# A hyena and gMLP encoder block on one core: ordinary products for the first two column pairs with the sine network as a background job, gate pairs and branch A last, and a last DFT step that multiplies standing data

## The chip, the cores and the metric
The kernel runs on one core of one Trainium2 chip. The metric is the device time of one execution in microseconds, lower is better. A core has a matrix engine (PE, whose loads of standing operands are listed as PEld), a vector engine (DVE), a scalar engine (ACT), a slower general engine (POOL), and SP, which here only issues transfers. Each engine takes its instructions in order.

## What is computed
One encoder layer on x of 2048 positions by 1024 channels:

```
h = rms_norm(x, pre_norm_w);  proj = h @ w_in            (1024 x 7168)
hy_in, hy_gate, sg_u, sg_v, sg_gate = split(proj)
A: x0, x1, v = split(short_conv(hy_in)); k = hyena_filter(...)   (a three layer sine network, times a decay)
   y_a = x0 * long_conv(v * x1, k, skip) * silu(hy_gate)         (by FFT)
B: y_b = sg_u * (sgu_w @ norm(sg_v) + sgu_b) * silu(sg_gate)     (per head and chunk of 128)
y = concat(y_a, y_b) @ w_out;  out = x + rms_norm(y, post_norm_w)
```

All is float32; the large products keep that accuracy by three passes with split operands (high parts and low parts).

## The kernel before
**Products.** The input and output products are cut into *pairs*: a pair takes two column blocks of 128 (two heads, or a gate with its operand) and half of the positions (h = 0 or 1, two chunks of 512). Each pair is a 2 by 2 block product done in Strassen's manner (the Winograd form): seven *units* u = 0 to 6, each a product of one combination of x (`self.X[u]`) and one combination of weights (a tile `wu`), each of 4 blocks times 3 passes: 84 matmuls of 128x512 a pair (`product`, `mm3`, lines 303 to 305 of the profile). `prep_begin` loads the two weight blocks as `wraw` and makes the combinations s1, s2, s3 (tiles `ws`, line 613); `prep_unit` makes high and low part of one unit's weights (lines 634 and 636); what is made in the first half of the positions is written to a spill (`WSB`, `WSU`, `WSG`, `WSV`) and read again in the second. `stream` runs the pairs in the order of `self.order`; the results leave PSUM in the `Take` classes.

**Order.** 72 pairs: for the first half of positions B (branch B's gate and operand), U (the two convolution inputs of branch A), V (branch B's values) mixed with G (branch A's gate); for the second half U, V mixed with G, B; then eight output pairs O for branch A (r = 0), whose sums go to `PT`, and eight for branch B (r = 1), which add them, normalise and write.

**Background.** Between the units, `tick` advances jobs; `background(jobs, rate)` starts so many a tick, with 3.5 ticks a pair. `x_phase` first normalises and turns the first half of x and makes all seven combinations; the sine network `mlp` stands ahead of the first pair in the program. Under the first eight pairs run the 32 filter jobs `k1_job` (decay, sums and differences, a first DFT step; lines 838 to 863, result `AK`), then `x_job` for the second half of x, `kfft_job`, `wo_job` (combinations of w_out, result `WT`), and under the second half's V, G and B pairs `fft_job` (two DFT steps and the product of the spectra, lines 1069 to 1085, result `BY`) and `inv_job` (the last step, lines 1101 to 1115, result `Y`). A scheduler then orders each engine's instructions; tiles come from pools with a fixed number of buffers for each tag, and a tile waits until the buffer's last user is done.

**The places that the change touches.** In `k1_job` the sums `s` have four buffers of their own (tag kq) and the evictions `ev` three. In `fft_jobs` the inverse jobs of the first channel half are mixed with the FFT jobs of the second. `inv_job` multiplies the table `g1`, standing, with the data (`b<-raw,g`, line 1107), copies the result on ACT (line 1109), turns it on PE (line 1113) and multiplies it on DVE with the gate (line 1114). When branch A's output pairs begin, `stream` lets all jobs end first (`turn`), since their weights are `Y`.

## Time and profile before

| | us |
|---|---|
| median of 3 runs | 2075.62 (2069.07 to 2076.07) |
| the profiled execution | 2072.21 |
| its span | 2070.2 |
| PE busy | 1904.2 (92%) |
| PE weight loads busy | 1414.1 (68%) |
| DVE busy | 1345.9 (65%) |
| ACT busy | 857.4 (41%) |
| POOL busy | 452.0 (22%) |

Matmuls are pipelined, so their times overlap and PE's busy share says little; the step from one start to the next says more. The transfers move 249 GB/s on the mean. A row of a group gives count, busy time, mean duration in ns, and the idle time of the engine ahead of the group with what ended it. A row of the table of stages gives a stretch, its length, and for each engine the busy time in it.

### The profile page before, as it was taken

Reading aid. Unit: us, or ns where it says so; the run is one execution under the profiler, and the core shown is the slowest. Engines: PE = TensorE matmul, PEld = TensorE weight load, DVE = VectorE, ACT = ScalarE, POOL = GpSimd, SP = SyncE. Lnnn points to the kernel's source line nnn. Section 1 sums busy time; section 2 is a strip of 40 time slices with the busy share of each in tenths; the row PEclk is TensorE's granted clock in tenths of the full one; section 3 lists DMA queues with packets and bytes.
Section 4 is the critical chain, followed back from the end, with each engine's and each line's share of the span. In section 5 each row is a group of like instructions: output and inputs, shape, how many; then the busy total and the mean of one; then the engine's idle time right before and its main releaser. Section 6 shows DMA issues by size and latency. Waiting matters only on the chain.

```text
span 2070.2 us, 23947 instructions
## 1 busy us (share of the span) xinstructions
PE 1904.2 (92%) x7832; PEld 1414.1 (68%) x7832; DVE 1345.9 (65%) x2070; ACT 857.4 (41%) x1540; POOL 452.0 (22%) x392
## 2 busy tenths in 40 slices
PE   4698899999999999899998999899999999999997
PEld 3465666777777777677776666566667777887776
DVE  6767878787755465745553888878672226536876
ACT  6344444565344443644444333233332224335443
POOL 4431322223212212121111111011011112323331
PEclk9899999999999999999999999899999999999999
DMA  8288777776687977998877797789898888536563
GB/s 272 105 262 268 244 247 259 232 261 242 237 292 233 342 227 272 324 281 256 274 247 234 243 303 258 218 281 286 273 294 291 280 268 290 188 102 244 193 213 132
DMA packets 330204, 515.91 MB, mean 249 GB/s; under 512 B 107451, under 2 KB 177339, under 8 KB 327359
## 3 DMA queue, kind: packets, MB, share of 16 engines
q1 hardware_dynamic: 263328, 439.58, 65.1%
q10 hardware_dynamic: 61856, 69.81, 9.9%
q0 software_dynamic: 4896, 4.98, 1.0%
q8 instruction: 63, 1.03, 0.2%
q14 instruction: 61, 0.50, 0.1%
HBM read 316.10 MB, written 204.48 MB: 251 GB/s over the span
## 4 chain that ended last, share of the span: by engine, by line
PE 33%; DVE 8%; DMA 6%; issue 2%; ACT 1%; POOL 1%; SPq 0%; DVEq 0%; ACTq 0%; POOLq 0%
PE proj L305 8%; PE proj L304 8%; PE proj L303 8%; PE b L1081 3%; PE b L1107 2%; PE b L1069 2%; DMA x<-WT 1%; DVE pb L1072 1%; DVE pa L1072 1%; DMA wraw<-Y 1%; DMA WT<-t 1%; DVE x L558 1%; DVE pa L1076 1%; PE b L996 1%; DVE wu L636 1%
## 5 line engine op out<-in xcount | busy, mean ns | idle before, releaser
L303 PE MATMUL proj<-x,wu 128*128 128x512 f32 x2016 | 833.0, 414 | 35.7 <-ACT sn L647 13.2
L304 PE MATMUL proj<-x,wu 128*128 128x512 f32 x2016 | 810.8, 402 | 12.8 <-DVE wu L636 10.3
L305 PE MATMUL proj<-x,wu 128*128 128x512 f32 x2016 | 807.6, 401 | 1.1 <-DVE x L558 0.6
L636 POOL TENSOR_TENSOR wu<-wraw,wu 128x512 fp32r<-128x512 f32 x172 | 262.3, 1525 | 1047.5 <-ACT wu L634 819.1
L303 PEld LDWEIGHTS proj<-x,wu 128*128 128x128 f32 x2016 | 383.6, 190 | 143.6 <-issue 33.7
L304 PEld LDWEIGHTS proj<-x,wu 128*128 128x128 f32 x2016 | 383.6, 190 | 118.2 <-issue 26.0
L305 PEld LDWEIGHTS proj<-x,wu 128*128 128x128 f32 x2016 | 383.4, 190 | 94.5 <-issue 13.5
L634 ACT CAST wu<-wraw 128x512 fp32r<-128x512 f32 x216 | 133.8, 620 | 285.5 <-PE proj L305 230.9
L636 DVE TENSOR_TENSOR wu<-ws,wu 128x512 fp32r<-128x512 f32 x176 | 129.8, 740 | 149.7 <-ACT wu L634 149.3
L634 ACT CAST wu<-ws 128x512 fp32r<-128x512 f32 x176 | 108.6, 620 | 219.5 <-PE proj L305 170.2
L647 ACT COPY sn<-proj 128x512 f32<-128x512 f32 x216 | 125.5, 581 | 109.5 <-PE proj L305 88.1
L1072 DVE TENSOR_TENSOR pa<-b,k 64x512 f32<-64x512 f32 x128 | 87.5, 683 | 51.2 <-PE b L1069 46.1
L613 POOL TENSOR_TENSOR ws<-wraw 128x512 f32<-128x512 f32 x44 | 80.3, 1825 | 161.1 <-DVE wu L636 113.1
L613 POOL TENSOR_TENSOR ws<-wraw,ws 128x512 f32<-128x512 f32 x44 | 59.4, 1350 | 220.9 <-DVE wu L636 212.5
L1072 DVE TENSOR_TENSOR pb<-b,k 64x512 f32<-64x512 f32 x128 | 88.9, 694 | 1.8
L1081 PE MATMUL b<-pa,tb 128*128 128x512 f32 x128 | 71.3, 639 | 14.4 <-DVE pa L1076 7.5
L1083 ACT COPY ev<-b 128x512 f32<-128x512 f32 x64 | 37.2, 585 | 108.0 <-PE b L1081 104.8
L613 DVE TENSOR_TENSOR ws<-wraw 128x512 f32<-128x512 f32 x44 | 40.4, 918 | 59.0 <-DMA wraw<-in_w_in_dram 24.9
L651 DVE TENSOR_TENSOR r<-proj,sn 128x512 f32<-128x512 f32 x64 | 43.8, 685 | 40.4 <-PE proj L305 39.6
L1069 PE MATMUL b<-raw,tu 128*128 128x512 f32 x128 | 66.0, 628 | 3.0 <-DMA raw<-AU 3.0
L861 PE MATMUL b<-s,ff 128*128 128x512 f32 x128 | 63.7, 613 | 5.0 <-ACT ev L863 2.3
L1032 PE MATMUL b<-raw,tk 128*128 128x512 f32 x128 | 63.6, 615 | 3.4 <-DMA raw<-AK 1.8
(169 smaller groups left out, 2234.8 us busy)
## 6 DMA issues: line engine op xcount, KB each, us to landing
wraw<-in_w_in_dram SPq DMA_DIRECT2D x84, 512.0 KB, 5.5
WSB<-wu SPq DMA_DIRECT2D x32, 512.0 KB, 4.9
dd<-in_c_dec_dram SPq DMA_DIRECT2D x32, 512.0 KB, 5.6
AK<-ev ACTq DMA_DIRECT2D x64, 256.0 KB, 4.2
WSU<-wu SPq DMA_DIRECT2D x32, 512.0 KB, 4.8
raw<-AK SPq DMA_DIRECT2D x32, 512.0 KB, 6.0
WSG<-wu SPq DMA_DIRECT2D x32, 512.0 KB, 6.3
KF<-ev ACTq DMA_DIRECT2D x32, 512.0 KB, 6.7
```

The source lines that it names most:

```text
L303: t.matmul(ps, sh, mh, start=first, stop=False, **kw)
L304: t.matmul(ps, sl, mh, start=False, stop=False, **kw)
L305: t.matmul(ps, sh, ml, start=False, stop=last, **kw)
L613: eng.tensor_tensor(t, x, y, op=op)
L634: nc.scalar.copy(w[:, 0], src[u])
L636: eng.tensor_tensor(w[:, 1], src[u], w[:, 0].bitcast(F32), op=ALU.subtract)
L647: self.nc.scalar.copy(s, ps)
L861: nc.tensor.matmul(ps, self.ff[:, d], s[d], start=True, stop=True)
L1032: nc.tensor.matmul(ps, tv[:, n], raw[:, n], start=True, stop=True)
L1069: nc.tensor.matmul(u, tv[0][:, n], raw[:, n], start=True, stop=True)
L1072: nc.vector.tensor_tensor(o, uu, kk, op=ALU.mult)
L1081: nc.tensor.matmul(ps, tv[1][:, n], prod[n], start=True, stop=True)
```

## The change
**First two pairs.** For the first two B pairs and the first half of positions the seven-unit product is replaced by the ordinary one: two block products for each output block, eight for a pair. `X[4]` and `X[6]` first hold the second chunk's plain blocks; the second pair's weights stand in `X[5]`'s place. The outputs go straight from PSUM through SiLU and a product to `UG`. What the second half needs of these pairs' combined weights is made apart (`first_sums`) from columns that are read a second time. `X[4]` and `X[5]` are filled afterwards. **Sine network.** It becomes one background job under the next two pairs, with a step after each layer's sine; the filter jobs follow under seven pairs, and `s`, `ev`, `wr`, `sk` share five buffers. **Order.** In the second half come U, then V mixed with B, then G, then the output pairs of branch B and last those of branch A. The FFT jobs run at 0.55 a tick, the inverse jobs all after them at 1.05, under the last G pairs and the branch B output pairs. **Last DFT step.** The data stand and the table moves, so the product comes out turned; the first PSUM bank, the ACT copy and the four turns go, and the gate tile moves from tag `ws` to `f`.

```diff
-        if self.h:
+        if not self.h:
             self.part = [self.b.o_load(2 * self.c + 1 - n) for n in range(2)][::-1]
...
-            self.order = B(0) + U(0) + GV(0) + U(1) + GV(1) + B(1) + O(0) + O(1)
+            self.order = B(0) + U(0) + GV(0) + U(1) + VB + G(1) + O(1) + O(0)
...
-                    self.nw_ = 3
+                    self.nw_ = 4
                     with self.pool("mlp") as ml:
-                        self.mlp(ml)
+                        self.background(iter([self.mlp(ml)]), 1.0)
+                        self.run(self.stream(2))
+                        self.rest()
                     with self.pool("k1") as kp:
-                        self.background(self.k1_jobs(kp), 1.4)
-                        self.run(self.stream(8))
+                        self.background(self.k1_jobs(kp), 1.6)
+                        self.run(self.stream(7))
...
-                    self.background(self.x_jobs(1), 0.25)
-                    self.run(self.stream(8))
+                    self.background(self.x_jobs(1), 0.32)
+                    self.run(self.stream(5))
...
-                    self.background(self.fft_jobs(), 1.0)
-                    self.run(self.stream(20, "w0"))
+                    self.background(self.fft_jobs(), 0.55)
+                    self.run(self.stream(20, "w1"))
+                    self.run(self.stream(8, "w0"))
...
+        def pair(n, chunk):
+            (b1, b2), c = ((0, 1), (4, 6))[chunk], self.order[n][2]
+            cols = slice(512 * chunk, 512 * chunk + 512)
+            sg, ps = None, None
+            for k in range(2):
+                ps = self.bank("proj")
+                self.product({0: X[b1]}, {0: w[n][2 * k]}, 0, ps, False)
+                yield
+                self.product({0: X[b2]}, {0: w[n][2 * k + 1]}, 0, ps, False, first=False)
+                if k == 0:
+                    sg = xs.tile([128, 512], F32, name="sg", tag="h", bufs=3)
+                    nc.scalar.activation(sg, ps, AF.Silu)
+                else:
+                    ug = xs.tile([128, 512], F32, name="ug", tag="h", bufs=3)
+                    nc.vector.tensor_tensor(ug, ps, sg, op=ALU.mult)
+                    nc.sync.dma_start(self.UG[c][:, cols], ug)
+                yield
...
+        for u, t, x, y, op in ((3, s1, a21, a22, ALU.add), (2, s2, s1, a11, ALU.subtract), (6, s1, a12, s2, ALU.subtract), (4, s2, a11, a21, ALU.subtract)):
+            tt(t, x, y, op=op)
+            spill(u, t)
+            yield
...
-        s = [kp.tile([128, 512], F32, name="s", tag="kq", bufs=4) for _ in range(2)]
+        s = [kp.tile([128, 512], F32, name="s", tag="kq", bufs=5) for _ in range(2)]
...
-            ev = kp.tile([128, 512], F32, name="ev", bufs=3)
+            ev = kp.tile([128, 512], F32, name="ev", tag="kq", bufs=5)
...
-        v = self.inv_jobs()
         for g in range(0, 32, 2):
             yield self.fft_job(g, 1)
-            if g > 6:
-                yield next(v)
-        for _ in range(4):
-            yield next(v)
-        yield iter(())
-        yield from v
+        for _ in range(2):
+            yield iter(())
+        self.rate = 1.05
+        yield from self.inv_jobs()
...
-        xg = self.product_tile("xg")
+        xg = self.f("xg")
...
-        ps = self.bank("b")
-        for d in range(2):
-            nc.tensor.matmul(ps, g1[:, d], raw[:, d], start=d == 0, stop=d == 1)
-        y = self.f("y")
-        nc.scalar.copy(y, ps)
-        yield
+
         ps = self.bank("a")
         for q in range(4):
-            nc.tensor.transpose(ps[:, q * 128:q * 128 + 128], y[:, q * 128:q * 128 + 128], self.ident)
+            sl = slice(q * 128, q * 128 + 128)
+            for d in range(2):
+                nc.tensor.matmul(ps[:, sl], raw[:, d, sl], g1[:, d], start=d == 0, stop=d == 1)
+        yield
```

On DVE, under the filter jobs, the program before had these rows (dd are the decayed columns, s their sum and difference, l their absolute sum, wu a weight's low part; in brackets the semaphores that a row waits for, DMAHW being transfers):

```order
L838 TENSOR_TENSOR dd<-a,dd 128x512 [waits PE_49]
L840 TENSOR_TENSOR s<-dd 128x512 [waits DVE_49]
L841 TENSOR_TENSOR s<-dd 128x512
L636 TENSOR_TENSOR wu<-ws,wu 128x512 [waits Activation_49]
L838 TENSOR_TENSOR dd<-a,dd 128x512 [waits DMAHW1_49,PE_49]
L843 TENSOR_TENSOR l_682<-l_682,dd 128x1024 [waits Activation_49]
```

The sums waited for DVE's own work alone, at all 64 places. In the changed program the same stretch of DVE reads:

```order
L947 TENSOR_TENSOR dd<-a,dd 128x512 [waits PE_49]
L949 TENSOR_TENSOR s<-dd 128x512 [waits DMAHW6_49,DMAHW0_49,DVE_49]
L950 TENSOR_TENSOR s<-dd 128x512 [waits PE_49]
L744 TENSOR_TENSOR wu<-ws,wu 128x512 [waits Activation_49]
L952 TENSOR_TENSOR l_1278<-l_1278,dd 128x1024 [waits Activation_49]
L947 TENSOR_TENSOR dd<-a,dd 128x512 [waits DMAHW2_49]
```

The buffer of a sum is now one that an eviction or a DFT product had, so 35 of the 64 sums wait for a transfer and others for PE. On PE, in the last DFT step, the program before had (proj products, b and a PSUM banks, pa and tb the second DFT step's operands, raw and tu the first one's):

```order
L303 MATMUL proj<-x_6863,wu 128x512
L1081 MATMUL b<-pa,tb 128x512
L1107 MATMUL b<-raw,g_10787 128x512 x2
L1069 MATMUL b<-raw,tu 128x512
L1113 MATMUL a<-ident,y 128x128 x4
L1069 MATMUL b<-raw,tu 128x512
L304 MATMUL proj<-x_6863,wu 128x512
```

The changed program has, under the branch B output pairs:

```order
L303 MATMUL proj<-x_13346,wu 128x512
L304 MATMUL proj<-x_13346,wu 128x512
L305 MATMUL proj<-x_13346,wu 128x512
L1217 MATMUL a<-g_13033,raw 128x128 x16
L303 MATMUL proj<-x_13374,wu 128x512
```

Sixteen rows of two jobs stand together, with no FFT row near them; the first stands after 4608 product matmuls of 6072, the last after 5328, and branch A's output pairs begin after 5400. On SP, where the second half's V pairs end, the changed program reads (VM is the mixed values' place in memory, vm the buffer that a B pair reads them into):

```order
L1078 DMA VM<-v_9324 128x1024 [waits DMAHW2_49,DVE_49]
L1070 DMA bi<-in_sgu_b_dram 128x128 [waits DMAHW3_49]
L713 DMA wraw<-in_w_in_dram 128x1024 [waits DMAHW4_49,Pool_49]
L174 DMA vm<-VM 128x1024 [waits DMAHW5_49,DMAHW2_49]
L738 DMA wu<-WSB_92 128x1024 [waits DMAHW6_49,PE_49]
```

The load of vm waits for the store three rows ahead of it (DMAHW2), whose buffer it takes; before, all V pairs of this half were over when the B pairs came.

More of the change, by code (lines that the diff above doesn't have):

```diff
@@ L440, in x_norm @@
         ss = xs.tile([128, 1], F32, name="ss", bufs=2)
-        jk = self.junk(xs)
+        jk = self.wide([128, D], "jk") if xs is self.fp else xs.tile([128, D], F32, name="jk")
         nc.scalar.activation(jk, xn, AF.Square, accum_out=ss)
@@ L485, in x_phase @@
             for i in range(4):
-                xts[c, i] = self.x_load(xs, 0, i, c, 4, nc.scalar if i % 2 else nc.sync)
+                xts[c, i] = self.x_load(xs, 0, i, c, 4, nc.scalar if i % 2 and not c else nc.sync)
                 if (c, i) == (0, 0):
                     nc.gpsimd.dma_start(pw, self.i["pre_norm_w"].partition_broadcast(128))
-                if (c, i) == (0, 3):
-                    self.next_w = self.prep_begin(0)
+                if (c, i) in ((0, 3), (1, 0)):
+                    self.first_weights(c)
         self.load_more()
+        X = self.X
+        hi = lambda u, i: X[u][:, 0, i]
+        lo = lambda u, i: X[u][:, 1, i]
         def put(u, src, i, eng):
-            hi, lo = self.X[u][:, 0, i], self.X[u][:, 1, i]
-            nc.scalar.copy(hi, src)
-            eng.tensor_tensor(lo, src, hi.bitcast(F32), op=ALU.subtract)
-        keep = {}
+            nc.scalar.copy(hi(u, i), src)
+            eng.tensor_tensor(lo(u, i), src, hi(u, i).bitcast(F32), op=ALU.subtract)
+        b11 = [self.rp.tile([128, 512], F32, name="b11", tag=t, bufs=n) for t, n in (("ws", 3), ("ws", 3), ("ws", 3), ("s1", 1))]
+        b21 = []
         for i in range(4):
@@ L504, in x_phase @@
                 put(half, ps, i, nc.vector)
-                keep[half, i] = xs.tile([128, 512], F32, name=f"b{half}", tag="b", bufs=8)
-                nc.scalar.copy(keep[half, i], ps)
+                if half:
+                    b21.append(xs.tile([128, 512], F32, name="b21", bufs=4))
+                    nc.vector.tensor_copy(b21[i], ps)
+                else:
+                    nc.scalar.copy(b11[i], ps)
+            if i == 1:
+                w = [self.first_split(0, [self.wp.tile([128, 2, 512], F32R, name="wu", tag="wu", bufs=5) for _ in range(4)])]
         for i in range(4):
@@ L509, in x_phase, with turn @@
                 self.x_norm(xs, xts[1, i], pw)
-            raw = lambda n: xs.tile([128, 512], F32, name=n, tag="t", bufs=4)
-            self.x_sums(raw, lambda u, src: put(u, src, i, nc.vector if u == 6 else nc.gpsimd), keep[0, i], keep[1, i], xts[1, i])
+        w.append(self.first_split(1, [X[5][:, :, k] for k in range(4)]))
+        t3 = []
+        def turn(i):
+            b12 = self.x_turn(xts[1, i], 0, "a")
+            put(4, b12, i, nc.vector)
+            t3.append(xs.tile([128, 512], F32, name="t3", bufs=4))
+            nc.scalar.copy(t3[i], b12)
+            t1 = xs.tile([128, 512], F32, name="t1", bufs=1)
+            tt(t1, b12, b11[i], op=ALU.subtract)
+            b22 = self.x_turn(xts[1, i], 1, "b")
+            put(6, b22, i, nc.vector)
+            t2 = xs.tile([128, 512], F32, name="t2", bufs=1)
+            tt(t2, b22, t1, op=ALU.subtract)
+            tt(t3[i], b22, t3[i], op=ALU.subtract)
+            tt(b21[i], b21[i], t2, op=ALU.subtract)
+            put(3, t1, i, nc.gpsimd)
+            put(2, t2, i, nc.gpsimd)
@@ new lines, in x_phase @@
+        turns = {1: 0, 3: 1, 5: 2, 6: 3}
+        n = 0
+        for p in range(2):
+            for _ in pair(p, 0):
+                if n in turns:
+                    turn(turns[n])
+                n += 1
+        for _ in pair(0, 1):
+            pass
+        sums = [self.first_sums(xs, k) for k in range(2)]
+        for g in sums:
+            next(g)
+        self.at = 2
+        self.next_w = self.prep_begin(2)
+        self.prep_unit(self.next_w)
+        for _ in pair(1, 1):
+            self.prep_unit(self.next_w)
@@ new lines, in x_phase, with first_weights @@
+        for u, t in ((4, t3), (5, b21)):
+            for i in range(4):
+                put(u, t[i], i, nc.vector)
+        for g in sums:
+            for _ in g:
+                pass
+    def first_weights(self, n):
+        raw = [self.rp.tile([128, 2, 512], F32, name="wraw", tag="wraw", bufs=3) for _ in range(2)]
+        for t, b in zip(raw, self.order[n][3:]):
+            self.nc.sync.dma_start(t, self.i["w_in"][b].rearrange("p (h k) c -> p h (k c)", h=2))
+        self.first = getattr(self, "first", []) + [raw]
@@ new lines, in first_split, with first_sums, spill @@
+    def first_split(self, n, out):
+        nc = self.nc
+        for k, w in enumerate(out):
+            src = self.first[n][k // 2][:, k % 2]
+            nc.scalar.copy(w[:, 0], src)
+            nc.gpsimd.tensor_tensor(w[:, 1], src, w[:, 0].bitcast(F32), op=ALU.subtract)
+        return out
+    def first_sums(self, xs, n):
+        nc, tt = self.nc, self.nc.vector.tensor_tensor
+        raw = []
+        for b in self.order[n][3:]:
+            raw.append(xs.tile([128, 2, 512], F32, name="xt", bufs=4))
+            nc.sync.dma_start(raw[-1], self.i["w_in"][b].rearrange("p (h k) c -> p h (k c)", h=2))
+        yield
+        a11, a12, a21, a22 = [t[:, k] for t in raw for k in range(2)]
+        def spill(u, t):
+            hi, lo = self.split(nc.vector, t, xs, "h", 3)
+            for r, part in enumerate((hi, lo)):
+                nc.sync.dma_start(self.WS[self.order[n][1:3]][SPILL.index(u), :, r], part.bitcast(F32))
+        s1 = xs.tile([128, 512], F32, name="t1", bufs=1)
+        s2 = xs.tile([128, 512], F32, name="t2", bufs=1)
+        for u, t, x, y, op in ((3, s1, a21, a22, ALU.add), (2, s2, s1, a11, ALU.subtract), (6, s1, a12, s2, ALU.subtract), (4, s2, a11, a21, ALU.subtract)):
+            tt(t, x, y, op=op)
+            spill(u, t)
+            yield
```

29 lines of the change are left out of this document (17 added, 12 removed).

## Prediction
> **What bounds the kernel now.** I read the run by stages first. The cuts were found with the timeline of the products: 345.3 is the end of the first eight pairs, 531 of the next eight, 1096.5, 1530.7 and 1738.1 begin the last three kinds, 1897.3 the last eight pairs. The columns are length, then busy time of PE, its weight loads, DVE, ACT and POOL.
> ```profile
> core 0: us, PE busy (x) PEld busy (x) DVE busy (x) ACT busy (x) POOL busy (x), PEclk, DMA share, GB/s
> 0.00:30.10 30.10, 9.70 (x40) 7.73 (x41) 14.47 (x22) 16.35 (x33) 4.88 (x7) 1.00 0.91 256
> 30.10:114.50 84.40, 57.46 (x211) 40.74 (x210) 65.06 (x101) 38.98 (x73) 41.02 (x25) 0.82 0.45 155
> 114.50:254.00 139.50, 122.09 (x436) 81.56 (x434) 107.48 (x141) 62.73 (x98) 38.12 (x41) 0.98 0.82 267
> 254.00:345.30 91.30, 85.39 (x315) 59.96 (x316) 72.16 (x96) 42.82 (x68) 21.93 (x22) 0.98 0.77 254
> 345.30:531.00 185.70, 171.94 (x755) 136.13 (x755) 142.06 (x161) 98.62 (x209) 55.03 (x63) 0.99 0.70 238
> 1096.50:1530.70 434.20, 411.79 (x1601) 276.22 (x1601) 336.28 (x630) 143.80 (x247) 50.39 (x44) 0.98 0.82 265
> 1530.70:1738.10 207.40, 207.01 (x862) 153.58 (x861) 75.95 (x104) 57.30 (x95) 31.45 (x24) 1.00 0.88 281
> 1738.10:1897.30 159.20, 154.84 (x673) 126.96 (x672) 82.22 (x103) 66.53 (x107) 47.47 (x32) 0.99 0.53 187
> 1897.30:2070.20 172.90, 154.61 (x673) 125.43 (x672) 132.87 (x157) 74.14 (x134) 51.69 (x30) 0.98 0.55 186
> sum 2070.20, PE 1904.16 PEld 1414.09 DVE 1345.89 ACT 857.41 POOL 451.98; mean PE 173.11 PEld 128.55 DVE 122.35 ACT 77.95 POOL 41.09
> ```
> Matmuls overlap, so PE's busy time hides what it loses; the timeline gives the step from one product matmul to the next where nothing is missing.
> ```profile
> 1937.13 0.39 PE L304 MATMUL proj<-x,wu 128*128 128x512 f32 x1
> 1937.36 0.39 PE L305 MATMUL proj<-x,wu 128*128 128x512 f32 x1
> ```
> That step is 0.227 us, so a pair of 84 costs 19.06 us. Eight pairs need 152.5 of the 159.2 us from 1738.1 on: those pairs are PE's, as are the 207.4 us ahead of them (PE busy 207.01). The first 114.5 us hold two pairs and the sine network, which need far less, and DVE is busy 65.06 of 84.4 us there. The stage from 1096.5 is the mixed one. So time can come from three places: the start, the stage from 1096.5, and PE's own work.
>
> **The start: two ordinary pairs, then the sine network under pairs 2 and 3.** Before, PE stands after the first two units:
> ```profile
> PE proj L303 <- ACT x L495: 13.1, 1, 13.1
> L444 DVE SCALAR_TENSOR_TENSOR xt<-xt,rs,pw 128x1024 f32<-128x1024 f32 x8 | 11.9, 1488 | 0.1
> L496 DVE TENSOR_TENSOR x<-b,x 128x512 fp32r<-128x512 f32 x7 | 4.8, 679 | 0.0
> 11.31 0.16 DVE L588 RECIPROCAL rs<-sd 128x1 f32<-128x1 f32 x1 [10.29 <-ACT sd L586]
> ```
> The wait of 13.1 us is for a combination of x. The first product cannot come sooner than the 30.1 us of now, since it takes all four blocks of unit 0. After that, ordinary products need only x itself. DVE has, until both halves of x are in, 8 norms (11.9), and by 0.68 us each 16 low parts, 16 sums and 4 copies (24.5), some 5 us of reciprocals, weights and gates: 41 us from 11.3, with some waits 56. PE does the first half of both pairs (96 x 0.227 = 21.8) from 30 at a clock that the second row puts at 0.82: to about 57. The second half takes it to about 80. Ordinary products cost 24 more matmuls, 5.4 us, which are in this. When is the filter stage reached? The order has the first filter matmul after 494 product matmuls; (494 - 192) x 0.227 = 69 more, and the sine network's few: 152. Is DVE ready by then? It had 14.5 + 65.1 = 80 us by 114.5, the sine network among them. The 16 operations for the spill, 4 copies and 8 low parts taken from POOL add 28 at 0.68 to 0.9 us, some 22; 14 weight operations of the first two pairs fall out, about 11; and 2.8 more pairs come, at 8.2 each (the two windows from 114.5 to 345.3 have 179.6 us for 6 pairs and 31 filter jobs of 4.2): 23. That makes 114 of 152, so yes; PE sets this part.
>
> On SP the moved step stands behind other things: the second reading of two pairs' columns (2 MB), the spills, and then the network's own 22 small loads. None of these is late for the network if SP is free by 80, and the queues moved 155 GB/s up to 114.5, 267 after it, so there is room for 2 MB. If the network's result comes 10 us late, the filter stage starts at 162 and the lead below shrinks by 10; I keep that for the range. What x loads go over SP instead of ACT costs nothing, hidden by the DVE chain on x; the inlined helper, the fourth wide buffer and the rate 0.32 likewise, hidden by PE.
>
> Where is the kernel before at the same progress? Line 305 is a third of the products, line 836 runs twice in each filter job (first two rows line 305, the others line 836):
> ```profile
> 30.10:114.50 84.40, 23.95 (x56) 11.57 (x56) 0.82 0.45 155
> 114.50:254.00 139.50, 40.58 (x98) 18.51 (x97) 0.98 0.82 267
> ...
> 114.50:254.00 139.50, 16.51 (x36) 6.88 (x36) 0.98 0.82 267
> 254.00:345.30 91.30, 15.60 (x26) 5.14 (x26) 0.98 0.77 254
> L838 DVE TENSOR_TENSOR dd<-a,dd 128x512 f32<-128x512 f32 x64 | 42.0, 683 | 25.5 <-DMA dd<-in_c_dec_dram 21.5 <-PE a L837 2.5 <-PE b L861 1.3
> L840 DVE TENSOR_TENSOR s<-dd 128x512 f32<-128x512 f32 x32 | 24.3, 758 | 0.5
> L843 DVE TENSOR_TENSOR l<-l,dd 128x1024 f32<-128x1024 f32 x32 | 42.6, 1331 | 12.9 <-ACT dd L842 12.9
> ```
> At 254 it has 3 x 154 = 462 product matmuls and 18 filter jobs behind it; the changed kernel, at 152, has none of those jobs. So it leads by 102 us and owes 18 jobs. Their price: at least 3.3 us each (254 to 345.3: 91.3 us less 213 products x 0.227, over 13 jobs), by DVE's own work (line 841 is line 840's twin) 2 x 0.683 + 2 x 0.758 + 1.331 = 4.2, and 5.3 if DVE stays at the 79% it has in that window. I take 4.2: 76 us. Three of the seven pairs that now carry them are convolution pairs, heavier for DVE; with the ring below I put 10 us for both. Lead left: 102 - 76 - 10 = **16 us**; from 45 (3.3 each, nothing else) to a loss of 5 (5.3 each, 12 us on top).
>
> **The filter's ring.** Sums and evictions now share five buffers (four and three before), so DVE's sums wait for the eviction's write, 35 of 64 times by the order, where none did. The present wait for that write falls on ACT:
> ```profile
> L863 ACT COPY ev<-b 128x512 f32<-128x512 f32 x64 | 36.3, 581 | 24.9 <-DMA AK<-ev 13.9 <-PE b L861 9.7 <-PE a L837 1.2
> AK<-ev ACTq DMA_DIRECT2D x64, 256.0 KB, 4.2
> ```
> 13.9 us in all; behind DVE's wait stand the weights' low parts and the evictions of the products. Half of it, 7 us, is in the sum; nothing to 32 x 4.2 = 134 us are its ends, nearer the small one, since a job comes every 7 us and the landing takes 4.2.
>
> **The last DFT step.** It loses two 512-column products, four turns and an ACT copy (off PE's path), and gains eight 128-column products:
> ```profile
> 1644.66 0.39 PE L305 MATMUL proj<-x,wu 128*128 128x512 f32 x1
> 1644.89 0.60 PE L1113 MATMUL a<-ident,y 128*128 128x128 f32 x4
> 1645.33 1.88 PE L1107 MATMUL b<-raw,g 128*128 128x512 f32 x4
> 1647.28 0.40 PE L304 MATMUL proj<-x,wu 128*128 128x512 f32 x1
> ...
> 1393.78 1.05 PE L996 MATMUL b<-sw,vn 128*128 128x128 f32 x8
> 1394.67 0.60 PE L979 MATMUL a<-ident,v 128*128 128x128 f32 x4
> 1393.78 0.86 PEld L996 LDWEIGHTS b<-sw,vn 128*128 128x128 f32 x7 [0.24 <-issue]
> L996 PEld LDWEIGHTS b<-sw,vn 128*128 128x128 f32 x256 | 41.5, 195 | 15.9 <-issue 8.7 <-PE proj L305 1.8 <-DVE vn L991 1.7
> ```
> Old: 1644.89 to 1647.05 (one product step ahead of 1647.28), 2.16 us. New: line 996 is the same form, 8 pieces in 0.89 us, so 16 take 1.78. 32 jobs x 0.38 = **12 us**, all on PE, which is what binds where they run. Seven loads fit into 0.86 us beside the matmuls, so they cost nothing; if they did not, see the rivals.
>
> **Gate pairs and branch A last.** The FFT jobs go from 3.5 to 1.9 a pair and stretch from some 11 pairs to 17.6; the inverse jobs run beside the last gate pairs and the branch B output pairs. PE's need of the 28 pairs is, before, 28 x 19.06 = 534, FFT 256 pieces of 0.43 (1.72 for line 1107's four) 110, inverse 69, the mixing and the leftover of line 924 some 32: 745 of 800.8 us. So 56 us are lost, about 47 ahead of 1530.7, where DVE has 336 us against PE's 388 (87%). An FFT job is ten DVE operations, 7.1 us:
> ```profile
> L1072 DVE TENSOR_TENSOR pb<-b,k 64x512 f32<-64x512 f32 x128 | 88.9, 694 | 1.8
> L1076 DVE SCALAR_TENSOR_TENSOR pa<-pb,sgn,pa 128x512 f32<-128x512 f32 x64 | 49.5, 773 | 0.2
> ```
> Spread over 17.6 pairs, DVE has about 375 us (336 and 76, less 22 of inverse work and 15 of the last gate pairs) against 477: 79%. Less dense but not slack; I take 48 us lost, **8 us** gained; ends: 35 (nothing lost but the branch turn) and a loss of 20, for the wait below. The turn from one output half to the other stays: all that the eight pairs from 1738.1 lose now, the turn among it, is 6.7 us, and in the new order the last inverse job stands 72 product matmuls (16 us) ahead of it, so no transfer of its 5 us should be late.
>
> Sum, against the execution's own 2072.2 us (span 2070.2): -16 - 12 - 8 = -36. The median of the runs, 2075.6, is 3.4 above it; from there **2040 us**.
>
> **The rivals.**
> More comes (0.15): the owed jobs cost 3.3 us and nothing else (-45), the mixed stage loses only 25 (-31), inverse -12: about 1990. For it: PE's need is that small. Against: DVE would have to be over 85% busy to 531, which no window shows.
> The start gives nothing (0.15): the owed jobs cost 5.3, the mixed stage keeps its loss: 2063.
> The store of V (0.07): the vm load takes a buffer whose store stands three rows ahead of it on SP; behind it wait the loads of spilled weights, for which PE waits, and DVE's gate product.
> ```profile
> VM<-v SPq DMA_DIRECT2D x8, 512.0 KB, 4.1
> vm<-VM SPq DMA_DIRECT2D x8, 512.0 KB, 6.3
> ```
> 10.4 us at each of two places, if nothing hides it: 2061.
> The ring decides (0.09): from a mean wait of 1.3 us a job on, 43 us in all instead of 7, it is slower than before; at half the landing, 2.1 us, 67 in all: 2100. For it: the new wait stands on the busiest engine behind PE. Against: 13.9 us is all that the same write costs now.
> Weight loads stand open (0.04): 16 loads of 0.195 us, 3.1, on top of 1.78 make 4.9 for the 2.16 of now; 32 jobs lose 88 us instead of gaining 12: 2140. The rows of line 996 speak against it: seven loads and eight matmuls share the same 0.9 us. The Trainium skill, "TensorE: Matmul & The Clock Gate", Part 3, The mechanism, speaks for it: a weight load overlaps running matmuls only when its row group differs, and these take all rows. By that rule the step would be a loss; the trace does not agree.
>
> **How the numbers follow.** 0.5 for the forecast, 2015 to 2062. Range 2000 to 2080: it leaves out half of the first rival (0.07) and the two slow ones (0.13). Over 0.5% (10 us, about what a measurement of this kernel can tell) faster: forecast, more, and over half of the 0.22 near 2062, 0.77; slower the two last, 0.13; the same 0.10.
>
> **What would show it.** First product near 30 us and no gap until 80; first filter job near 150; branch U done near 515. Inverse jobs of 1.8 us on PE. Over 1.3 us a job of DVE waiting for AK, or loads of line 1217 outside the matmuls, or PE losing over 75 us in the last 36 pairs, would make it wrong.

## The result and the profile after

| | before | after |
|---|---|---|
| median, us | 2072.35 (2068.44 to 2076.07, 4 runs) | 2021.59 (2019.64 to 2028.06, 4 runs) |
| profiled span, us | 2070.2 | 2020.4 |
| PE busy, us | 1904.2 (92%) | 1886.5 (93%) |
| DVE busy, us | 1345.9 (65%) | 1349.0 (67%) |
| ACT busy, us | 857.4 (41%) | 829.7 (41%) |

The ratio is 0.976, with a 95% interval of 0.974 to 0.978: some 50 us faster. Forecast were 36, to 2040, with a range of 2000 to 2080.

The stages of the changed kernel, with the columns of the table in the prediction. The rows begin at the start, at the first product (26.6), at the first filter job's matmul (163.8), and then where the kernel has done as many product matmuls as the kernel before at the end of 16, 28, 36, 48, 56 and 64 pairs (its own count is 24 higher, for the ordinary pairs). The cut at 80.0 is the prediction's.
```profile
core 0: us, PE busy (x) PEld busy (x) DVE busy (x) ACT busy (x) POOL busy (x), PEclk, DMA share, GB/s
0.00:26.60 26.60, 7.82 (x32) 6.27 (x32) 13.12 (x20) 15.72 (x33) 7.33 (x9) 1.00 0.90 235
26.60:80.00 53.40, 53.35 (x243) 44.54 (x244) 43.52 (x60) 30.04 (x57) 23.64 (x17) 1.00 0.80 271
80.00:163.80 83.80, 75.44 (x302) 57.44 (x301) 63.68 (x101) 33.42 (x59) 20.64 (x18) 0.94 0.61 201
163.80:504.60 340.80, 311.73 (x1202) 222.19 (x1201) 279.12 (x347) 176.31 (x326) 88.20 (x108) 0.97 0.77 258
504.60:844.00 339.40, 319.20 (x1345) 238.61 (x1344) 193.17 (x406) 148.06 (x276) 71.58 (x65) 0.98 0.83 275
844.00:1072.90 228.90, 210.19 (x934) 165.65 (x934) 128.47 (x161) 109.18 (x209) 38.06 (x41) 0.99 0.89 280
1072.90:1433.40 360.50, 347.68 (x1451) 250.65 (x1450) 266.03 (x529) 109.58 (x184) 48.75 (x37) 1.00 0.81 258
1433.40:1642.10 208.70, 204.52 (x852) 152.57 (x851) 135.14 (x185) 69.92 (x126) 35.17 (x32) 0.99 0.84 266
1642.10:1847.30 205.20, 201.94 (x1092) 174.02 (x1091) 92.70 (x122) 63.80 (x104) 43.06 (x31) 0.99 0.75 247
1847.30:2020.40 173.10, 154.63 (x673) 125.31 (x671) 134.09 (x157) 73.71 (x133) 49.46 (x30) 0.98 0.61 207
```
PE is busy without a gap from 26.6 to 80 (53.35 of 53.40 us, at the full clock); before, it had 57.46 of the 84.4 us from 30.1. Between 80 and 163.8 it waits 8.4 us. Its longest wait there is 4.89 us, and the products behind it start about 0.43 us apart instead of 0.227 for some 5 us (some rows of this place: start, duration, and in brackets idle time ahead and what ended it):
```profile
91.79 0.39 PE L305 MATMUL proj<-x,wu 128*128 128x512 f32 x1
94.89 0.62 ACT L296 CAST hi<-t 128x512 fp32r<-128x512 f32 x1 [2.00 <-DMA WSB<-lo]
95.63 0.69 DVE L298 TENSOR_TENSOR lo<-t,hi 128x512 fp32r<-128x512 f32 x1 [1.67 <-ACT hi L296]
96.24 0.68 DVE L759 TENSOR_TENSOR sg<-proj,sn 128x512 f32<-128x512 f32 x1
97.07 0.77 PE L303 MATMUL proj<-x,wu 128*128 128x512 f32 x1 [4.89 <-DVE w L852]
99.56 0.63 PE L303 MATMUL proj<-x,wu 128*128 128x512 f32 x1
99.98 0.63 PE L304 MATMUL proj<-x,wu 128*128 128x512 f32 x1
```
The view names a short memset (w, line 852). Just ahead of it stands a gate product that reads a product's bank (line 759), behind a low part for the spill of the first pairs' weights (line 298), which waited by way of ACT for a write of that spill. So a write of that spill, which the prediction did not count as holding PE up, seems to do so here; who released PE is inferred.

Two stages that the change did not mean to touch answer to these rows of the kernel before:
```profile
531.00:860.10 329.10, 316.68 (x1346) 237.68 (x1346) 187.53 (x402) 146.60 (x273) 71.00 (x64) 0.98 0.83 275
860.10:1096.50 236.40, 212.66 (x933) 168.10 (x932) 129.78 (x162) 109.54 (x210) 38.98 (x41) 0.97 0.87 274
```
The first half's V and G pairs (329 us before) now take 339.4, and the second half's U pairs after them (236.4) take 228.9. At equal progress, counted by product matmuls, the whole run compares so:

| us | before | after | gain |
|---|---|---|---|
| to the first product | 30.1 | 26.7 | 3.4 |
| from there to the 470th (first filter job of after) | 227.9 | 137.1 | 90.8 |
| to the end of 16 pairs | 273.0 | 340.9 | -67.9 |
| first half's V and G, 12 pairs | 329.0 | 339.4 | -10.4 |
| second half's U, 8 pairs | 236.5 | 228.8 | 7.7 |
| the 28 pairs that follow | 800.8 | 774.4 | 26.4 |
| last 8 pairs and the end | 172.9 | 173.1 | -0.2 |
| sum | 2070.2 | 2020.4 | 49.8 |

So half of the gain is there when 16 pairs are done (26.3), and half comes from the 28 pairs with the FFT and the inverse jobs.

The last DFT step on PE, a piece of the timeline (start, duration, engine, line):
```profile
1607.51 0.39 PE L305 MATMUL proj<-x,wu 128*128 128x512 f32 x1
1607.73 1.95 PE L1217 MATMUL a<-g,raw 128*128 128x128 f32 x16
1609.43 0.48 PE L303 MATMUL proj<-x,wu 128*128 128x512 f32 x1
1609.75 0.40 PE L304 MATMUL proj<-x,wu 128*128 128x512 f32 x1
```
The last two rows are one product step apart as a rule, 0.227; taken back from 1609.75 the product at 1609.43 would have stood at 1609.52, so the sixteen rows hold PE from 1607.73 to 1609.52, 1.79 us. They are one job: each of its eight products shows as two rows in the trace. (The sixteen rows of the program shown ahead of the prediction are two jobs; in the trace two jobs stand together at one place only, and at the other 30 a job stands alone.) The group of their weight loads, from the page:
```profile
L1217 PEld LDWEIGHTS a<-g,raw 128*128 128x128 f32 x512 | 62.8, 194 | 3.7 <-DVE ws L721 1.4
```
Sixteen loads of 0.194 us are 3.1 us on the record, overlapping one another (all 512 cover 62.8 us, 1.96 a job), and PE goes on after 1.79: they lie beside the matmuls. The Trainium skill, "TensorE: Matmul & The Clock Gate", Part 3, The mechanism, would have a load overlap running matmuls only when its row group differs; these loads and matmuls take all 128 rows, and this case does not agree. (The Trainium skill, "TensorE: Matmul & The Clock Gate", Part 2, Step-by-step, also lets a load run ahead of matmuls if it goes to the background weight buffer. That would fit the rows; no row shows which buffer a load goes to.)

The first filter matmul stands at 163.6 (the line's matmuls, shortest, median and longest in ns, first and last start):
```profile
L945 PE MATMUL a<-hi,gd x64: 389/397/799, 163.6 to 387.1; 128*128 128x512 f32 x64
```

The filter's ring (the five buffers that sums, evictions and weight loads share): what the second sum (line 950) and then the evictions (line 972) waited for, of the changed kernel; a row is waited-for thing, us in total, times.
```profile
L950 DVE TENSOR_TENSOR s<-dd x32: 675/684/2105, 172.9 to 393.3; 128x512 f32<-128x512 f32 x32
its engine sat idle before it (us, times) until:
  DMA AK<-ev: 1.5, 4
```
```profile
L972 ACT COPY ev<-b x64: 568/587/609, 175.7 to 407.7; 128x512 f32<-128x512 f32 x64
  PE b L970: 11.4, 14
  DMA AK<-ev: 6.2, 2
```
DVE lost 1.5 us to the write; the first sum (line 949) lost nothing to it, and ACT lost 6.2 where it had lost 13.9. The load of vm, last:
```profile
L1114 DVE TENSOR_TENSOR ug<-ug,vm x16: 678/692/1609, 1180.0 to 1440.8; 128x512 f32<-128x512 f32 x16
  DMA vm<-VM: 1.5, 2
```

### The profile page after: what moved, and what is told of

It is laid out like the page before. It is cut to its first block, busy times and chain, and to the rows that moved or that the text cites. A ratio compares the mean times of both kernels' runs of the same rounds, so it can differ in the third digit from the quotient of the medians.

```text
span 2020.4 us, 24531 instructions
## 1 busy us (share of the span) xinstructions
PE 1886.5 (93%) x8112; PEld 1437.2 (71%) x8112; DVE 1349.0 (67%) x2082; ACT 829.7 (41%) x1500; POOL 425.9 (21%) x384
## 5 line engine op out<-in xcount | busy, mean ns | idle before, releaser
L303 PE MATMUL proj<-x,wu 128*128 128x512 f32 x1992 | 825.3, 415 | 25.9 <-ACT sn L755 9.2
L304 PE MATMUL proj<-x,wu 128*128 128x512 f32 x1992 | 799.6, 401 | 9.4 <-DVE wu L744 8.4
L305 PE MATMUL proj<-x,wu 128*128 128x512 f32 x1992 | 798.1, 401 | 0.0
L303 PEld LDWEIGHTS proj<-x,wu 128*128 128x128 f32 x1992 | 379.2, 190 | 130.7 <-issue 31.8
L744 POOL TENSOR_TENSOR wu<-wraw,wu 128x512 fp32r<-128x512 f32 x168 | 245.1, 1459 | 1019.3 <-ACT wu L742 869.2
L304 PEld LDWEIGHTS proj<-x,wu 128*128 128x128 f32 x1992 | 380.0, 191 | 110.2 <-issue 22.5
L305 PEld LDWEIGHTS proj<-x,wu 128*128 128x128 f32 x1992 | 378.9, 190 | 90.6 <-issue 12.7
L742 ACT CAST wu<-wraw 128x512 fp32r<-128x512 f32 x210 | 129.7, 620 | 286.6 <-PE proj L305 241.4
L744 DVE TENSOR_TENSOR wu<-ws,wu 128x512 fp32r<-128x512 f32 x168 | 117.8, 703 | 146.6 <-ACT wu L742 139.6
L742 ACT CAST wu<-ws 128x512 fp32r<-128x512 f32 x168 | 103.6, 620 | 267.7 <-PE proj L305 231.0
L721 POOL TENSOR_TENSOR ws<-wraw 128x512 f32<-128x512 f32 x42 | 72.6, 1728 | 136.3 <-DVE wu L744 100.1
L970 PE MATMUL b<-s,ff 128*128 128x512 f32 x128 | 62.8, 608 | 8.2 <-DVE s L966 2.5
L1217 PEld LDWEIGHTS a<-g,raw 128*128 128x128 f32 x512 | 62.8, 194 | 3.7 <-DVE ws L721 1.4
```

The lines of the kernel that those rows point to most:

```text
L303: t.matmul(ps, sh, mh, start=first, stop=False, **kw)
L304: t.matmul(ps, sl, mh, start=False, stop=False, **kw)
L305: t.matmul(ps, sh, ml, start=False, stop=last, **kw)
L721: eng.tensor_tensor(t, x, y, op=op)
L742: nc.scalar.copy(w[:, 0], src[u])
L744: eng.tensor_tensor(w[:, 1], src[u], w[:, 0].bitcast(F32), op=ALU.subtract)
```

## The experiments

All twelve were timed against the kernel before, in five rounds; a ratio is to it, with its 95% interval.

**The three parts alone, and each left out.** The start is the new first two pairs with the sine network as a job, the shared ring and the rates that go with it; order is the order of the pairs with the FFT and inverse rates and the gate tile's move to tag f; the step is the last DFT step.

The step alone, in the kernel before:
```diff
-        ps = self.bank("b")
-        for d in range(2):
-            nc.tensor.matmul(ps, g1[:, d], raw[:, d], start=d == 0, stop=d == 1)
-        y = self.f("y")
-        nc.scalar.copy(y, ps)
-        yield
...
+            for d in range(2):
+                nc.tensor.matmul(ps[:, sl], raw[:, d, sl], g1[:, d], start=d == 0, stop=d == 1)
```


> The kernel before with the new last DFT step alone (data standing, table moving, no turns, no copy). Theory: the step costs 1.78 instead of 2.16 us of PE time a job and PE binds where most of the jobs run, so 12 us less than before, ratio 0.994. Rival: weight loads stand open, 88 us more, ratio 1.042. Rival: part of the jobs run in the stage that DVE binds, so only 5 to 8 us less, ratio 0.997.

Measured: 2066.91 us, 0.9971 (0.9953 to 0.9989), as the second rival said. The rows of the first twelve and the next eight of the 28 pairs, to be held against the rows from 1096.5 and 1530.7 in the prediction (434.2 and 207.4 us):
```profile
1096.60:1537.20 440.60, 409.99 (x1682) 284.46 (x1680) 339.05 (x630) 138.45 (x237) 49.69 (x44) 0.98 0.81 262
1537.20:1736.00 198.80, 198.33 (x1038) 167.92 (x1037) 80.32 (x107) 46.30 (x75) 31.96 (x24) 1.00 0.91 295
```
In the old order 22 of the 32 inverse jobs run where PE binds (198.33 of 198.80 us busy). There the shorter step gives 8.6 us, and 22 x 0.37 is 8.1. The other ten stand in the stage ahead, which got no shorter: PE's busy time falls by 1.8, DVE's rises by 2.8, and the stage is 6.4 us longer. The same pair of kernels with the new start says the same: 8.9 us less where PE binds (207.8 to 198.9), 2.6 more in the stage ahead (428.9 to 431.5). Both pairs of traces say that the step gives nothing in the mixed stage; one trace of a stage is good to a few us only, and why the stage grew stays open.

The order alone:
```diff
-            self.order = B(0) + U(0) + GV(0) + U(1) + GV(1) + B(1) + O(0) + O(1)
...
+            self.order = B(0) + U(0) + GV(0) + U(1) + VB + G(1) + O(1) + O(0)
...
-                    self.background(self.fft_jobs(), 1.0)
-                    self.run(self.stream(20, "w0"))
+                    self.background(self.fft_jobs(), 0.55)
+                    self.run(self.stream(20, "w1"))
+                    self.run(self.stream(8, "w0"))
```


> The kernel before with the new order and rates alone (V with B, then G, branch B output pairs, branch A last; FFT jobs at 0.55, inverse jobs after them), with the old start and the old last DFT step. Theory: what PE loses from the second half's V pairs to branch A's output pairs falls by about 10 us, ratio 0.995. Rival: the old DFT step and the FFT jobs use the banks and buffers of the output pairs and nothing is gained, ratio 1.000.

Measured: 2068.46, 0.9975 (0.9961 to 0.9989), between the theory and the rival. In its profile the 28 pairs gain 9.5 us (791.3 for 800.8), as the theory said, and the first half's V and G pairs, which it does not touch, lose 3.2.

The start alone:
```diff
-            self.seen = set()
+            self.seen = {p[1:3] for p in self.order[:2]}
...
-                        self.mlp(ml)
+                        self.background(iter([self.mlp(ml)]), 1.0)
+                        self.run(self.stream(2))
+                        self.rest()
...
-                        self.background(self.k1_jobs(kp), 1.4)
-                        self.run(self.stream(8))
+                        self.background(self.k1_jobs(kp), 1.6)
+                        self.run(self.stream(7))
```


> The kernel before with the new start alone (ordinary products for two pairs, sine network as a job, filter jobs under seven pairs, shared ring). Theory: 27 us gained at the end of the first 16 pairs, as in the changed kernel's trace, and kept: ratio 0.987. Rival: the stage of the first half's V and G pairs gives back about 13 us, because its schedule shifts with the start: ratio 0.993.

Measured: 2046.98, 0.9871 (0.9849 to 0.9893), as the theory said.

The changed kernel without the start, the edit above turned round:
```diff
-            self.seen = {p[1:3] for p in self.order[:2]}
+            self.seen = set()
...
-                        self.background(iter([self.mlp(ml)]), 1.0)
-                        self.run(self.stream(2))
-                        self.rest()
+                        self.mlp(ml)
```


> The changed kernel with the old start: new order and new last DFT step together. The two alone gave 0.9975 and 0.9971. Theory: together they give what the changed kernel's trace shows from the second half's V pairs on, 22 to 27 us, ratio 0.988, since only in the new order do all inverse jobs run where PE binds. Rival: they add, 11 us, ratio 0.9946, and the rest of the changed kernel's gain is between the start and one of them.

Measured: 2050.9, 0.9888 (0.9867 to 0.991), as the theory said.

Without the new order and rates:
```diff
-                    self.background(self.fft_jobs(), 0.55)
-                    self.run(self.stream(20, "w1"))
-                    self.run(self.stream(8, "w0"))
+                    self.background(self.fft_jobs(), 1.0)
+                    self.run(self.stream(20, "w0"))
```


> The changed kernel with the old order and rates from the second half's V pairs on. Theory: start and step add, 0.9871 x 0.9971 = 0.984, 16 us more than the changed kernel. Rival: the order is worth only its 5 us, ratio 0.979.

Measured: 2040.74, 0.9841 (0.9821 to 0.986), as the theory said.

With the old last step:
```diff
-            for d in range(2):
-                nc.tensor.matmul(ps[:, sl], raw[:, d, sl], g1[:, d], start=d == 0, stop=d == 1)
-        yield
...
+        ps = self.bank("b")
+        for d in range(2):
+            nc.tensor.matmul(ps, g1[:, d], raw[:, d], start=d == 0, stop=d == 1)
+        y = self.f("y")
+        nc.scalar.copy(y, ps)
```


> The changed kernel with the old last DFT step. Theory: the old step costs 0.38 us of PE a job and, in the new order, its copy and its second bank as well: 15 to 20 us more than the changed kernel, ratio 0.984. Rival: 6 us more, as the step gave alone, ratio 0.979.

Measured: 2034.67, 0.9815 (0.9794 to 0.9835), by the ratios 11 us more than the changed kernel and so between the theory and the rival. Its last eight of the 28 pairs, where 205.2 us stand in the changed kernel:
```profile
1637.30:1857.10 219.80, 214.15 (x890) 157.77 (x889) 93.40 (x125) 79.88 (x132) 44.46 (x32) 0.99 0.71 238
```
PE is 214.15 us busy there instead of 201.94, and the stage is 14.6 us longer. Of these, 27 jobs of 0.37 are 10, and PE's waits in the stage are 5.6 us instead of 3.2; the rest is open. Over all 28 pairs it is 11.6: 786.0 against 774.4.

Together the eight kernels give a table (ratio; the 28 pairs in us at equal progress):

| | old step | new step |
|---|---|---|
| old start, old order | 1 (800.8) | 0.9971 (797.4) |
| old start, new order | 0.9975 (791.3) | 0.9888 (773.0) |
| new start, old order | 0.9871 (795.4) | 0.9841 (789.2) |
| new start, new order | 0.9815 (786.0) | 0.976 (774.4) |

In us of 2072.35: the start is worth 26.7 alone, 27 with the step, 33 with the order and 26.5 last of the three (0.9888 to 0.976), so within the noise it adds to the other two. The step is worth 6 in the old order, 18 and 11 in the new; the order 5 and 12 with the old step, 17 and 17 with the new. Order and step together are 23. An interval is about 4 us to each side, and that of a difference of two ratios about 6. So the pattern is shown, not each figure: with the old start the step gives clearly more in the new order (18 for 6); with the new start the 11 for 6 are within the noise, though the 28 pairs say the same (11.6 for 6.2).

**The sine network written out ahead of the third and fourth pair, instead of a job under them.**
```diff
-                        self.background(iter([self.mlp(ml)]), 1.0)
+                        for _ in self.mlp(ml):
+                            pass
                         self.run(self.stream(2))
-                        self.rest()
```


> The changed kernel with the sine network written out ahead of pairs 2 and 3 instead of being a job under them. Theory: the scheduler mixes engines anyway, but DVE takes the network's 31 us in one stretch, so PE waits there; about 10 us more than the changed kernel, ratio 0.981 to before. Rival: the job form gives nothing, ratio 0.976.

Measured: 2027.39, 0.9767 (0.9747 to 0.9788), not to be told from the change itself; the theory's 10 us did not come. The 470th product comes 9 us later (146.1 after the first, not 137.1), and 4.3 of them are back when 16 pairs are done (336.6 us from there, not 340.9). That the network is a job is not what brings the start's gain. What is left is the two ordinary pairs, the network's place behind them, the ring and the rates, and no run parts these.

**The FFT jobs dense again, the inverse jobs where they are now** (28 more empty places keep their start).
```diff
-                    self.background(self.fft_jobs(), 0.55)
+                    self.background(self.fft_jobs(), 1.0)
...
-        for _ in range(2):
+        for _ in range(30):
             yield iter(())
```


> The changed kernel with the FFT jobs at 1.0 a tick (3.5 a pair, as before) and 30 empty places behind them, so that the inverse jobs start about where they do in the changed kernel. Theory: the thinner FFT jobs are what the new order gains from; at the old density DVE binds the first nine pairs again, 10 to 15 us more than the changed kernel, ratio 0.982. Rival: the density does not matter, since total DVE and PE work are the same: ratio 0.976.

Measured: 2041.5, 0.9847 (0.9826 to 0.9867). The 28 pairs in three rows, which answer to the rows from 1072.9, 1433.4 and 1642.1 of the changed kernel:
```profile
1073.90:1495.40 421.50, 396.65 (x1534) 269.91 (x1533) 332.90 (x630) 124.56 (x208) 49.32 (x37) 0.98 0.82 266
1495.40:1660.20 164.80, 164.80 (x785) 138.57 (x784) 66.78 (x83) 57.83 (x103) 33.42 (x32) 1.00 0.71 222
1660.20:1864.30 204.10, 200.23 (x1075) 172.14 (x1074) 94.48 (x122) 63.28 (x103) 45.08 (x32) 0.99 0.74 246
```
The first inverse job stands after 4584 product matmuls (4608 in the changed kernel), so its start was kept. The first row holds all 32 FFT jobs here and 21 in the changed kernel, so single rows are not to be compared, only the sum. In the first row DVE has 332.90 of 421.50 us (79%), in the changed kernel 266.03 of 360.50 (74%). The sum is 790.4 against 774.4 with the same instructions, so the 16 us are a matter of density; and the kernel with the start and the step in the old order stands at 789.2, and at 0.9841 in all. By the prediction's way of counting (28 x 19.06 + 110 + 32 x 1.79 + 32 = 733) 57 us are lost here, 41 in the changed kernel, and 56 were lost before: the new order without the thin FFT jobs saves nothing.

**The jobs for the second half of x earlier.** In the changed kernel three of the 28 writes of these jobs' results (XS) stand in the V and G pairs, where none stood before (transfers issued from 503.6 to 845.5: count, size, time to landing).
```profile
XS<-t SPq DMA_DIRECT2D x2, 256.0 KB, 3.0
XS<-b SPq DMA_DIRECT2D x1, 256.0 KB
```
```diff
-                    self.background(self.x_jobs(1), 0.32)
+                    self.background(self.x_jobs(1), 0.45)
```


> After with the four jobs for the second half of x started at 0.45 a tick instead of 0.32, so that the last of them ends inside the five pairs it runs under (before they had eight pairs at 0.25 and left no write behind; after, three of the 28 writes of XS stand in the next stage). The first half's twelve V and gate pairs take 339.4 us from product to product in after and 329.0 in before; the loss comes in the first six of them. Theory (the tail of the x jobs spills into that stage): those twelve pairs fall back to about 330, the run to about 2013. Rival (the stage is longer for another reason, such as the place at which its own jobs meet the pairs, or its transfers): the twelve pairs stay at 338 to 341 and the run within 4 us of after.

Measured: 2033.68, 0.9805 (0.978 to 0.9829), 9 us slower than the changed kernel by the ratios. No write of XS was left in the V and G pairs, and they still took 337.2 us. The eight pairs ahead of them took 246.8, not 238.2, and the U pairs behind 236.9, not 228.8. What PE waited for in the V and G pairs, first in the changed kernel, then here (us, times, longest):
```profile
PE a L1089 <- DVE v L759: 7.8, 3, 3.2
PE b L1142 <- DMA raw<-AK: 5.3, 4, 2.2
PE proj L303 <- DVE v L759: 2.2, 1, 2.2
```
```profile
PE a L1089 <- DVE v L759: 10.3, 3, 4.5
PE b L1142 <- DMA raw<-AK: 6.5, 6, 2.7
PE proj L303 <- DVE v L759: 1.8, 1, 1.8
```
The waits are no smaller. The theory falls: it is not the tail of the x jobs.

**FFT jobs thinner still**, with the x jobs as in the kernel before this.
```diff
-                    self.background(self.fft_jobs(), 0.55)
+                    self.background(self.fft_jobs(), 0.5)
...
-        self.rate = 1.05
+        self.rate = 1.15
```


> After with the x jobs at 0.45 as in the kernel beside it, the FFT jobs at 0.5 a tick instead of 0.55 and the inverse jobs at 1.15 instead of 1.05, so that both still end ahead of branch A's output pairs. Thinning the FFT jobs from 1.0 to 0.55 was worth 16 us in the 28 pairs (790.4 against 774.4). If what is left there (40 us more than the matrix engine's need) still goes by the density of FFT jobs, another 10% thinner gives some 3 to 6 us beside the kernel with the x rate alone. Rival: the rest is spread over the inverse jobs and the mixing, and the denser inverse jobs or a late last one cost as much: no difference, or up to 5 us slower.

Measured: 2035.76, 0.9823 (0.9798 to 0.9847), no difference from the kernel beside it; the 28 pairs take 771.2 against 773.0. The rows of these pairs, first in the kernel beside it, then here:
```profile
1084.40:1444.50 360.10, 351.19 (x1458) 252.82 (x1456) 264.43 (x532) 108.89 (x185) 49.42 (x37) 1.00 0.81 262
1444.50:1650.10 205.60, 202.46 (x863) 152.13 (x861) 128.69 (x180) 66.97 (x120) 31.73 (x31) 1.00 0.84 268
1650.10:1857.40 207.30, 200.66 (x1075) 172.41 (x1075) 97.31 (x124) 64.58 (x106) 44.09 (x32) 0.98 0.72 241
```
```profile
1086.30:1440.70 354.40, 343.16 (x1441) 250.60 (x1440) 250.57 (x512) 104.34 (x179) 49.02 (x37) 1.00 0.80 255
1440.70:1642.80 202.10, 199.12 (x783) 144.38 (x782) 140.59 (x194) 68.07 (x123) 32.46 (x31) 1.00 0.83 261
1642.80:1857.50 214.70, 210.70 (x1169) 182.40 (x1168) 101.76 (x130) 69.30 (x110) 44.82 (x32) 0.99 0.80 263
```
The first two rows get 9.2 us shorter and the last one 7.4 longer, with 31 inverse jobs in it instead of 26: five jobs of 1.79 are 9. So work was moved and hardly any time gained; since both rates changed together, no run shows what the thinner FFT jobs would give alone.

**The ring parted, and the ring narrower.**
```diff
-        s = [kp.tile([128, 512], F32, name="s", tag="kq", bufs=5) for _ in range(2)]
+        s = [kp.tile([128, 512], F32, name="s", tag="kq", bufs=3) for _ in range(2)]
...
-            ev = kp.tile([128, 512], F32, name="ev", tag="kq", bufs=5)
+            ev = kp.tile([128, 512], F32, name="ev", bufs=2)
```


> After with the filter's five shared buffers parted again, in the same space: three for sums and weight loads, two for the evictions. None of the 64 sums then waits for a transfer (35 do in after); the evictions wait for their own two. If the ring decides nothing (theory: the vector engine's waits for the write of the evictions are 1.5 us in all in after), the run stays within 4 us of after, and the stage with the filter jobs within 3. Rival (the ring costs by order, not by the waits that the profile names): 5 to 15 us faster than after in that stage. Going the other way, two buffers for the evictions may put the wait on the scalar engine.

Measured: 2016.75, 0.9727 (0.9705 to 0.9749). That is the lowest time of all kernels here, 5 us under the changed one, and the intervals barely meet (0.974 to 0.9749). In the stage with the ring little is gained: at the end of 16 pairs it stands at 502.7 us against 504.6. The rest lies in the V and G pairs (332.3 us against 339.4). Their code is the same, but PE takes it in another order there than in the changed kernel. Whether the 5 us come of the edit, by way of that order, is not shown.
```diff
-        s = [kp.tile([128, 512], F32, name="s", tag="kq", bufs=5) for _ in range(2)]
+        s = [kp.tile([128, 512], F32, name="s", tag="kq", bufs=4) for _ in range(2)]
...
-            ev = kp.tile([128, 512], F32, name="ev", tag="kq", bufs=5)
+            ev = kp.tile([128, 512], F32, name="ev", tag="kq", bufs=4)
```


> After with four shared buffers in the filter's ring instead of five: 44 of the 64 sums wait for a transfer by the order, instead of 35. The prediction's rival had a price of 1.3 to 2.1 us of wait a job from which the ring decides. If a job comes every 10 us or so and a write lands in 4.4, five buffers are more than enough and four nearly so: 0 to 8 us slower. If the ring is at its edge: 20 us or more slower, with the vector engine's waits for that write over 30 us in all.

Measured: 2023.86, 0.9769 (0.9745 to 0.9794), the same as with five. DVE now stands at the first sum, six times, until a write has landed:
```profile
L949 DVE TENSOR_TENSOR s<-dd x32: 676/686/1785, 169.2 to 391.2; 128x512 f32<-128x512 f32 x32
its engine sat idle before it (us, times) until:
  DMA AK<-ev: 9.1, 6
```
Even 9.1 us of waiting, 0.3 a job, move the end of 16 pairs by 1.2 us only (505.8 against 504.6). The ring has room: with five buffers a write lands in 4.4 us (before 4.2), and 32 jobs spread over the 220 us of line 950's row come 7 us apart.

## Why the prediction held, point by point

- **The start: 16 forecast, 26 measured.** The mechanism was right, two terms were not. The prediction ruled out a first product sooner than 30.1 us; it came at 26.7 (26.3 to 27.6 in the ten kernels with the new start), and what brought it forward was not tried apart. PE runs from the first product on without a gap to 80, with 211 products done where 192 were forecast. The first filter matmul came at 163.6 all the same, not 152: the 283 products up to it need 64.2 us, PE waits 8.4 (at a clock of 0.94 from 80 to 163.8), the network's matmuls take 6, and 5 go into products further apart than 0.227 us, as behind the wait of 4.89. At the 470th product the kernel leads by 258.0 - 163.8 = 94 us, where 102 was forecast. The owed jobs cost less: the way from there to the end of 16 pairs is 67.9 us longer for the 18 jobs, 3.8 each with the ring and the heavier pairs in it (3.6 to 4.0 in the five kernels that have the same code up to there), where 76 + 10 = 86 were put down, 4.8 each. That term was mis-sized: I added DVE's own work for a job (4.2) as if it were all on the path, but DVE is busy 279.12 of 340.80 us there (82%, more than any of the prediction's rows up to 531 showed) and PE 311.73 (91%). What the prediction held against cheap jobs, that DVE would have to be over 85% busy, was thus nearly what happened. So the first rival's low price, 3.3, was nearer than the 4.8 of the sum. (The lead at that price, written as 45, is 102 - 18 x 3.3 = 43.)
- **The order: 8 forecast; the step: 12.** Together 20, and 26.4 in the 28 pairs of the profile, 23 by the ratios. The losses of the 28 pairs went from 56 to 41 us, not to 48. The step is 1.79 us for 2.16, as forecast to 0.01, and 32 x 0.37 = 12. Each alone, the order gives 5 and the step 6 by the ratios, 9.5 and 3.4 in the 28 pairs: there the order gives what was forecast, and the step does not. The prediction's clause "all on PE, which is what binds where they run" is true of the new order only; in the old one ten of the 32 inverse jobs stand in the mixed stage, which got no shorter. In the new order the old step costs more than its own 0.37 us a job: the last eight of the 28 pairs are 14.7 and 15.9 us shorter with the new step, for 27 and 26 jobs, where 10 would be the step's own; PE's waits give some 2 of the rest. The prediction left that out.
- **The two stages between.** They were put at nothing. The V and G pairs lose 10.4, the U pairs behind them gain 7.7. In the four kernels with the old start the V and G pairs take 328.9 to 332.2 us, in the ten with the new one 332.3 to 341.2; the two stages together 562.9 to 568.2 and 562.9 to 574.4. So the new start gives back some 5 us there on the mean. The tail of the x jobs is not the cause. The traces leave a lead: in the V and G pairs PE takes the same instructions in one order in all four kernels with the old start, and in another in seven of the ten with the new one (334.8 to 341.2 us). Only the three kernels in which the ring was parted or the x jobs' rate changed have other orders (332.3, and 337.2 and 334.3). So the schedule may be what costs there, or the ring by way of it; no run tests that, and the cause stays open.
- **The turn between the output halves** stayed as it was, 172.9 and 173.1 us for the last eight pairs and the end.
- **The rivals.** The ring did not decide (1.5 us of DVE's waits, and no price to be seen even at four buffers). The store of V cost 1.5 us of DVE's time, not 10.4 twice. Weight loads did not stand open. The start gave more than nothing, and "more comes" was right for the owed jobs, though not for the mixed stage: the 28 pairs kept 41 us of loss, not 25.

## What to carry to other kernels

Work that can be put off from a starved start is paid back at the price that it has where it goes: here that was 3.8 us for a job with 4.2 us of DVE's work, so the moved work's own durations are an upper guess where the engine still has gaps (DVE was 82% busy). A saving on one engine counts only in the stages that this engine sets, so ask first where the saved instructions run; here the same edit gave 6 us in one order of the work and 11 to 18 in another. Thin out the background jobs in the stage that loses most, and look at each step whether the time is gained or only moved to the next stage.

## What the hardware showed that was not expected

- With the data standing, a product comes out turned at almost no cost to PE: the sixteen 128-column rows of a job, each with a weight load of its own, take 1.79 us, 0.112 each, where the four 512-column rows that did the same multiplications took 1.72 and the turns came on top.
- The same twelve V and G pairs, with the same code and the same order on PE, take 334.8 to 341.2 us in seven traces, at a granted clock of 0.98 in the changed kernel. Five of these kernels have the same code from the first line to the end of these pairs, and the two ends of the range are among them. So one trace can't settle a difference of a few us in a stage, and a gain of 5 us that shows up in an untouched stage (as with the parted ring) can't be booked to the edit without more runs.
- A wait can cost PE more than its own length: behind the one of 4.89 us the products started about 0.43 us apart instead of 0.227 for some 5 us, with a granted clock of 0.88 from 80 to 100 us. That is one place, not a rule.
